# First layer of an MLP's last three parts as seven half-size products per pair of output tiles, on one Trainium2 core

## The chip, the cores and the metric

The kernel runs on one NeuronCore of one Trainium2 (trn2) chip. The metric is device time in microseconds (us) of one execution, smaller being better. The kernel before was timed three times: 862.24 us in the median, 861.46 to 862.5 us.

## What is computed

One inference step of a one-layer hybrid encoder, for a prompt of 512 tokens and a sample of 64 tokens (576 tokens together, 1024 channels): a modulated norm, an input projection, sparse attention beside a convolution, an output projection with a residual, and then the MLP, which is all that the change touches:

```
h = rms_norm(x, norm2_g) * (1 + sc2) + sh2
x = x + g2 * (jnp.square(jax.nn.relu(h @ w_ff1)) @ w_ff2)
...
y = rms_norm(x, final_g)
```

w_ff1 is 1024 x 4096, w_ff2 is 4096 x 1024, and sc2, sh2 and g2 come from the conditioning, one value per channel for the prompt and one for the sample. Everything is float32.

## The kernel before

**Float32 as three products.** A float32 operand is split into a high part, which is the value rounded to the matmul's 32-bit format (a copy on ScalarE, ACT), and a low part, the difference (a subtraction). A product is then three matmuls: high by high, high by low, low by high (`mm3`, lines 289 to 292). Matmul lines 290 to 292 therefore carry nearly all of the TensorE (PE) work.

**Layout.** Channels lie on the partitions, tokens along the free dimension, in two halves of 288 tokens (`JS`). An output tile is 128 channels by 288 tokens and takes one PSUM bank. Eight banks are shared out by tag: three `acc`, two `lg`, one `av`, which the MLP uses in rotation (`p_ff`), and two `tp`.

**The MLP in four parts.** Each part takes 1024 of the 4096 hidden channels. The first layer (`first_layer`, `ff1`, `ff1_evac`) makes eight hidden tiles: per tile 8 blocks of channels, 3 matmuls each, for two token halves, so 48 matmuls; the second layer makes eight output tiles from the eight hidden tiles, again 48 matmuls each, and adds them into the residual `x1` (`residual`, line 1087). In the last part the second layer runs over 320 and then 256 tokens, with the final norm behind it.

**Normalization folded behind the product.** The first layer multiplies the not yet normalized operand `h2` (the residual times the channel's scale). `h2` carries two extra columns with the shift, so one half has 290 columns. The evacuation then multiplies by the token's scale `rbc` on VectorE (DVE, line 1262), applies the shift as a bias in the ReLU on ACT (line 1266), squares into PSUM on ACT (line 1267), and makes high and low parts of the hidden tile `a` on DVE (lines 110 and 115).

**Weights.** `fetch` (line 318) issues a 512 KB DMA from SyncE (SP) into one of three `wraw` buffers, in the fixed sequence `order`. `split` (line 325) makes the high part in two copies of 128x512 on ACT (line 106) and the low part in two subtractions of 128x512 on GpSimd (POOL, line 332); `whi` and `wlo` have two buffers each. `take` fetches one tile, hands out a tile that is ready and splits the next one.

**What sets the order.** In the MLP the order of PE, ACT, DVE and POOL is the order in which the program is written (a manual schedule); each engine runs its own instructions in that order and waits for what it needs. The evacuation defers its last steps through `owed` and `settle`.

Of the kernel before, what the change touches and what calls it, by code (L numbers as in the profile page):

```python
# [7 lines left out]
FT = mybir.dt.float32  # L8
FR = mybir.dt.float32r
# [47 lines left out]
def f(ap):  # L57
    return ap.bitcast(FT)


def pump(g, n):
    for _ in range(n):
        next(g, None)
# [8 lines left out]
def step_kernel(ctx: ExitStack, tc: tile.TileContext, io):  # L72
# [25 lines left out]
    def p_tp():  # L98
        return bank("tp", 2)
# [14 lines left out]
    def sub(eng, out, a, b):  # L114
        eng.tensor_tensor(out, a, b, op=OP.subtract)
# [199 lines left out]
        order += [f_rows(w_ff2, 128 * KP * part, 128 * m) for m in range(NK)]  # L315
    stay = []

    def fetch():
        if order:
            raw = wgt.tile([128, 1024], FT, name="wraw", tag="wraw", bufs=3)  # L320
            src = order.pop(0)
            nc.sync.dma_start(raw.rearrange("p (k c) -> p k c", k=src.shape[1]), src)
            raws.append(raw)

    def split():
        if raws:
            raw = raws.pop(0)
            hi, lo = stay.pop(0)() if len(stay) > len(raws) + len(order) else [
                wgt.tile([128, 1024], FR, name=nm, tag=nm, bufs=2) for nm in ("whi", "wlo")]
            for c in (slice(0, 512), slice(512, 1024)):  # L330
                copy_to(act, hi[:, c], raw[:, c])
                behind[0] = pool.tensor_tensor(lo[:, c], raw[:, c], f(hi[:, c]), op=OP.subtract).ins  # L332
            ready.append((hi, lo))

    def take():
# [846 lines left out]
    ffp = new_pool(late, "ff")  # L1182

    def ft_(shape, dt, name):
        return ffp.tile(shape, dt, name=name, tag="d", bufs=21)

    mlp = ExitStack()
    mlp.enter_context(tc.manual_schedule(engines={mybir.EngineType.PE, mybir.EngineType.Activation, mybir.EngineType.DVE,
# [12 lines left out]
    def settle():  # L1201
        while owed:
            owed.pop(0)()
# [31 lines left out]
    def weight():  # L1235
        return [w.rearrange("p (k c) -> p k c", k=NK) for w in take()]
# [8 lines left out]
    def ff1(ts, parts=(range(NK),)):  # L1245
        w = weight()
        for ks in parts:
            for j in (1, 0):
                if j not in ts:
                    ts[j] = p_ff()[:, :HALF + 2 * j]  # L1250
                group(ts[j], w, h2, JX[j], ks)
            yield
# [21 lines left out]
        half(0)  # L1274
        return a

    def first_layer(part):
        a_ = []
        if part == 0:
            t0, t1 = {}, {}  # L1280
            g = ff1(t0, (FRONT, LAST))
            scales = spread(s2, 1.0 / D, rbc, dg)
            next(g)
            pump(scales, 1)
            pump(g, 2)
            pump(ff1(t1), 2)
            pump(scales, 2)
            a_ += [ff1_evac(t0), ff1_evac(t1)]
        while len(a_) < KP:
            t = {}  # L1290
            pump(ff1(t), 2)
            a_.append(ff1_evac(t))
        settle()
        return a_

# [7 lines left out]
            residual(t, r, m, G2)  # L1303

    for part in range(NP_ - 1):
        a_ = first_layer(part)
        for m in range(NK):
            ws = {m: weight()}
            if m == 0:
                second_layer(ws, (m,), a_, JS[::-1])  # L1310
            else:
                for r in JS:
                    t = p_ff()[:, :HALF]
                    group(t, ws[m], a_, r, range(NK))
                    residual(t, r, m, G2)

    def kept(m):
        if m < 4:
            return [big.tile([128, 1024], FR, name="wl", tag="b") for _ in range(2)]
        return [ft_([128, 1024], FR, "wl") for _ in range(2)]  # L1320
    stay += [lambda m=m: kept(m) for m in range(NK)]
    a_ = first_layer(NP_ - 1)


    fg = ft_([128, D], FT, "fg")
# [33 lines left out]
    for m in range(2, NK):  # L1359
# [1 line left out]
        t = p_ff()[:, :320]  # L1361
        group(t, ws[m], a_, LS[0], range(NK))
        residual(t, LS[0], m, G2)
    ys = [big.tile([128, D], FT, name="y", tag="b") for _ in range(2)]
    for m in range(NK):
        t = p_ff()[:, :TOK - 320]
        group(t, ws[m], a_, LS[1], range(NK))
# [43 lines left out]
```

## Time and profile before

| what | value |
|---|---|
| median of three runs | 862.24 us |
| the profiled execution's own time | 860.36 us |
| its span, first to last instruction | 858.6 us |
| PE busy, share of span | 94% |
| DVE, ACT, POOL busy | 52%, 48%, 35% |
| mean granted TensorE clock | 0.973 |

The profiled execution is one run on the chip; its time is 1.76 us more than its span and 1.88 us less than the median. Busy times are sums of instruction durations with overlaps counted once; matmuls are pipelined, so a matmul's own duration is longer than the distance from one to the next. A row of a group gives line, engine, operation, output and input with shapes, count, then busy time, mean duration, and the idle time of the engine before it with what ended it.

### The profile page before, as it was taken

How to read it: one execution, taken by the hardware profiler on the slowest of the kernel's cores; microseconds unless marked ns; L12 is line 12 of the kernel's file. 1: busy time of each engine (PE TensorE's matmuls, PEld its weight loads, DVE VectorE, ACT ScalarE, POOL GpSimd, SP SyncE). 2: the span in 40 equal slices, each digit the busy share in tenths (PEclk: the TensorE clock that was granted, in tenths of full speed). 3: DMA queues.
4: the chain of work that ended last, by engine and by line, in shares of the span. 5: the costliest groups of instructions: out<-in, count | busy, mean ns of one | idle time of the engine just before them, and what ended most of it. 6: DMA issues, size and time to landing. Idle time of an engine off the chain costs nothing.

```text
span 858.6 us, 17186 instructions
## 1 busy us (share of the span) xinstructions
PE 808.2 (94%) x6787; PEld 753.0 (88%) x6787; DVE 449.0 (52%) x1148; ACT 412.5 (48%) x976; POOL 303.5 (35%) x337
## 2 busy tenths in 40 slices
PE   5998997989798999999999999999999999999995
PEld 3797895567777988989999999999999999999995
DVE  4569879999997444654934311343113321144142
ACT  5365554555776787754745411443224522244332
POOL 0146342222244414232424343343433343343800
PEclk8799999899999999999999999999999999999998
DMA  8984157247343343732222323223222323223312
GB/s 241 309 205 123 53 146 184 60 100 187 112 113 110 116 137 115 222 122 77 74 74 75 97 76 93 80 75 99 74 77 82 88 83 90 74 74 101 120 55 57
DMA packets 164555, 95.57 MB, mean 111 GB/s; under 512 B 7699, under 2 KB 161119, under 8 KB 164475
## 3 DMA queue, kind: packets, MB, share of 16 engines
q1 hardware_dynamic: 164475, 94.48, 39.2%
q8 instruction: 53, 0.87, 0.4%
q14 instruction: 27, 0.22, 0.1%
HBM read 88.82 MB, written 5.64 MB: 110 GB/s over the span
## 4 chain that ended last, share of the span: by engine, by line
PE 69%; DVE 17%; ACT 7%; DMA 3%; issue 3%; POOL 1%; SPq 0%; ACTq 0%; DVEq 0%; POOLq 0%
PE ps_acc L290 11%; PE ps_acc L291 11%; PE ps_acc L292 11%; PE ps_lg L292 5%; PE ps_lg L290 5%; PE ps_lg L291 5%; DVE yc L564 3%; PE ps_av L292 3%; PE ps_av L290 2%; PE ps_av L291 2%; DVE score L690 2%; DVE m L688 2%; PE ps_tp L234 2%; DMA ada<-w_ada 1%; PE ps_av L887 1%
## 5 line engine op out<-in xcount | busy, mean ns | idle before, releaser
L332 POOL TENSOR_TENSOR wlo<-wraw,whi 128x512 fp32r<-128x512 f32 x172 | 222.6, 1314 | 378.3 <-ACT whi L106 378.0
L290 PE MATMUL ps_acc<-h,whi 128*128 128x288 f32 (+1 forms) x608 | 190.8, 314 | 0.0
L291 PE MATMUL ps_acc<-h,whi 128*128 128x288 f32 (+1 forms) x608 | 181.7, 299 | 0.0
L292 PE MATMUL ps_acc<-h,wlo 128*128 128x288 f32 (+1 forms) x608 | 181.1, 298 | 0.0
L106 ACT ACTIVATE whi<-wraw 128x512 fp32r<-128x512 f32 x172 | 99.8, 621 | 126.4 <-issue 120.6
L290 PEld LDWEIGHTS ps_acc<-h,whi 128*128 128x128 f32 x608 | 116.2, 191 | 14.3 <-issue 12.4
L291 PEld LDWEIGHTS ps_acc<-h,whi 128*128 128x128 f32 x608 | 116.7, 192 | 0.8
L292 PEld LDWEIGHTS ps_acc<-h,wlo 128*128 128x128 f32 x608 | 116.3, 191 | 0.0
L1266 ACT ACTIVATE z<-z,bs 128x224 f32<-128x224 f32 (+2 forms) x96 | 40.2, 450 | 98.6 <-DVE z L1262 98.6
L1087 DVE SCALAR_TENSOR_TENSOR x<-ps_acc,mod,x 128x288 f32<-128x288 f32 (+3 forms) x91 | 36.2, 420 | 83.6 <-PE ps_acc L292 83.0
L564 DVE SCALAR_TENSOR_TENSOR yc<-u,cw,yc 128x606 f32<-128x606 f32 x60 | 58.4, 981 | 0.6
L292 PE MATMUL ps_acc<-a,wlo 128*128 128x288 f32 x192 | 56.7, 295 | 0.0
L290 PE MATMUL ps_acc<-a,whi 128*128 128x288 f32 x192 | 56.6, 295 | 0.0
L291 PE MATMUL ps_acc<-a,whi 128*128 128x288 f32 x192 | 56.6, 295 | 0.0
L292 PE MATMUL ps_lg<-h,wlo 128*128 128x288 f32 (+1 forms) x176 | 52.2, 296 | 0.8 <-POOL wlo L332 0.8
L291 PE MATMUL ps_lg<-h,whi 128*128 128x288 f32 (+1 forms) x176 | 52.2, 297 | 0.0
L290 PE MATMUL ps_lg<-h,whi 128*128 128x288 f32 (+1 forms) x176 | 52.2, 296 | 0.1
L747 ACT ACTIVATE gc<-sful,sg 128x544 bf16<-128x544 f32 x48 | 35.8, 746 | 28.6 <-DVE sg L745 27.8
L872 POOL TENSOR_SCALAR prob<-prob,mx 128x128 f32<-128x128 f32 (+3 forms) x32 | 20.2, 631 | 56.8 <-DVE mx L871 34.2
L1087 DVE SCALAR_TENSOR_TENSOR x<-ps_lg,mod,x 128x64 f32<-128x64 f32 (+4 forms) x34 | 12.7, 407 | 52.5 <-PE ps_lg L292 52.5
L292 PE MATMUL ps_lg<-a,wlo 128*128 128x288 f32 x128 | 37.8, 295 | 0.0
L290 PE MATMUL ps_lg<-a,whi 128*128 128x288 f32 x128 | 37.8, 295 | 0.0
(358 smaller groups left out, 2019.0 us busy)
## 6 DMA issues: line engine op xcount, KB each, us to landing
wraw<-w_ff SPq DMA_DIRECT2D x64, 512.0 KB
ada<-w_ada SPq DMA_DIRECT2D x44, 512.0 KB
wraw<-w_in SPq DMA_DIRECT2D x24, 512.0 KB
wraw<-w_out SPq DMA_DIRECT2D x8, 512.0 KB
rep<-ud SPq DMA_DIRECT2D x24, 115.0 KB
xtok<-x_prompt SPq DMA_DIRECT2D x4, 512.0 KB
ada<-w_ada SPq DMA_DIRECT2D x8, 256.0 KB
ct<-cache_k SPq DMA_DIRECT2D x8, 256.0 KB
```

What stands on the lines that cost most here:

```text
L106: act.activation(out, in_, AF.Copy, scale=1.0 if scale is None else scale)
L234: pe.matmul(t[r:r + 32, :w], lhsT=cs[:, 4 * kh + kk, :], rhs=operand(v, kh, kk), start=kk == 0, stop=kk == 3, tile_position=(0, r))
L290: pe.matmul(out, lhsT=hi, rhs=src[:, 0, cs_], start=first, stop=False)
L291: pe.matmul(out, lhsT=hi, rhs=src[:, 1, cs_], start=False, stop=False)
L292: pe.matmul(out, lhsT=lo, rhs=src[:, 0, cs_], start=False, stop=last)
L332: behind[0] = pool.tensor_tensor(lo[:, c], raw[:, c], f(hi[:, c]), op=OP.subtract).ins
L564: dve.scalar_tensor_tensor(yc[c], src, w, yc[c], op0=OP.mult, op1=OP.add)
L688: dve.max(m, score[i])
L747: act.activation(eq, sful, AF.Sign, bias=cands[:, z:z + 1], scale=-1.0, accum_out=cnts[:, z:z + 1])
L872: pool.tensor_scalar(pt[:, :n], pt[:, :n], m[:, 1:2], 1.0, op0=OP.mult, op1=OP.mult)
L1087: dve.scalar_tensor_tensor(xm[:, a:b], t[:, a - r.start:b - r.start], mod[:, g, s, m:m + 1], xm[:, a:b], op0=OP.mult, op1=OP.add)
L1266: act.activation(y, y, AF.Relu, bias=bs[:, s:s + 1])
```

## The change

Of the four parts, the first keeps the old first layer, and the other three use a new one, `fast_layer`.

**Operands.** While part 0's first layer runs, `normalize` makes the normalized, scaled and shifted operand in float32 for four pairs of channel blocks (block i and block i+4). While part 0's second layer runs, `operands` forms, from each pair's four quarters (two channel blocks by two token halves), seven combinations: `11`, `12`, `22` are quarters, `s1` to `s4` sums and differences, each with high and low part. They stay in SBUF to the end.

**Products.** An output pair of tiles (256 hidden channels) by 576 tokens is computed as seven products of half size instead of eight (Strassen, in Winograd's form). A product is 4 channel blocks by 3 matmuls of 288 columns, 12 matmuls; a pair is 84. Products accumulate in banks `bk[0]`, `bk[1]`, `bk[4]`; some partial results are also added by DVE into other ones (`y3`, `u2`, a fourth bank `bk[5]`), and four half tiles come out, each through `made`: ReLU and square in place in PSUM, a high copy to SBUF, all on ACT, and a low subtraction on DVE.

**Weights.** `bring` takes two raw weight tiles, copies a quarter to a `tp` bank; `sums` makes four sums or differences on DVE (128x512, one operand in PSUM); `block` makes the high part of a product's weight on ACT and the low part on POOL (4 of 7) or DVE (3 of 7), three products ahead. A product's weight tile lies in one of four buffers.

**Other edits.** In part 0 a third tile's matmuls and its weight split are issued before the second tile is evacuated. Raw weight tiles also go to spare buffers (`spare`). Some splits make their second half's low part on DVE. The buffers of tag `d` go from 21 to 23, and some tiles of the last part change pools.

The diff, cut to what matters:

```diff
-                behind[0] = pool.tensor_tensor(lo[:, c], raw[:, c], f(hi[:, c]), op=OP.subtract).ins
+                behind[0] = (second[0] if c.start else pool).tensor_tensor(lo[:, c], raw[:, c], f(hi[:, c]), op=OP.subtract).ins
...
-        return ffp.tile(shape, dt, name=name, tag="d", bufs=21)
+        return ffp.tile(shape, dt, name=name, tag="d", bufs=23)
...
+    def normalize(i):
+        full[i] = ft_([128, 2, TOK], FT, "full")
+        for z in range(2):
+            m, y = i + 4 * z, full[i][:, z]
+            dve.tensor_tensor(y, x1[m // 2][:, m % 2], rbc, op=OP.mult)
+            for r, s in ((slice(0, SEQ), 0), (S, 1)):
+                act.activation(y[:, r], y[:, r], AF.Identity, scale=mod[:, SC2, s, m:m + 1], bias=mod[:, SH2, s, m:m + 1])
+    def operands():
+        for n, o in enumerate(OPS):
+            ops[o] = [big.tile([128, 2, TOK], FR, name="op", tag="b") if 2 * n + e < 9 else ft_([128, 2, TOK], FR, "op")
+                      for e in range(2)]
+        for i in range(4):
+            a11, a21 = full[i][:, 0, JS[0]], full[i][:, 0, JS[1]]
+            a12, a22 = full[i][:, 1, JS[0]], full[i][:, 1, JS[1]]
+            t = ft_([128, 4, HALF], FT, "sums")
+            c = slice(HALF * (i % 2), HALF * (i % 2) + HALF)
+            def put(o, src):
+                x = ops[o][i // 2]
+                copy_to(act, x[:, 0, c], src)
+                sub(dve, x[:, 1, c], src, f(x[:, 0, c]))
+            dve.tensor_tensor(t[:, 0], a21, a22, op=OP.add)
+            sub(dve, a21, a11, a21)
+            sub(dve, t[:, 1], t[:, 0], a11)
+            sub(dve, t[:, 2], a12, t[:, 1])
+            yield
+            put("11", a11)
+            put("12", a12)
+            yield
+            put("22", a22)
+            put("s3", a21)
+            yield
+            put("s1", t[:, 0])
+            put("s2", t[:, 1])
+            put("s4", t[:, 2])
+            yield
+    def bring(q):
+        b0, b1 = raws.pop(0), raws.pop(0)
+        x = p_tp()
+        copy_to(act, x, b1[:, :512])
+        pairs[q] = [b0[:, :512], b0[:, 512:], b1[:, :512], b1[:, 512:], x]
+    def sums(q, n):
+        if n == 2:
+            pairs[q].append(p_tp())
+        b11, b21, b12, b22, x, *y = pairs[q]
+        out, u, v = ((b12, b22, x), (x, x, b11), (y and y[0], b22, x), (y and y[0], b21, y and y[0]))[n]
+        sub(dve, out, u, v)
+    def block(g):
+        q, b = g // 7, g % 7
+        b11, b21, b12, b22, x, y = pairs[q] if len(pairs[q]) == 6 else pairs[q] + [None]
+        src = (b11, y, b21, b12, x, y, b22)[b]
+        nm = ("whi", "wlo")[g % 2]
+        w = blocks[g] = wgt.tile([128, 1024], FR, name=nm, tag=nm, bufs=2).rearrange("p (z c) -> p z c", z=2)
+        copy_to(act, w[:, 0], src)
+        return lambda: sub(dve if b in (1, 4, 5) else pool, w[:, 1], src, f(w[:, 0]))
+    MOVING = ("11", "s2", "12", "s3", "s1", "22", "s4")
+    def early(n):
+        if n == 0:
+            bring(0)
+            sums(0, 0)
+            sums(0, 1)
+        else:
+            sums(0, 2)
+            for g in range(2):
+                block(g)()
+    def made(q, a, r):
+        act.activation(q, q, AF.Relu)
+        act.activation(q, q, AF.Square)
+        copy_to(act, a[:, 0, r], q)
+        owed.append(lambda: sub(dve, a[:, 1, r], q, f(a[:, 0, r])))
+    def fast_layer():
         a_ = []
-        if part == 0:
-            t0, t1 = {}, {}
-            g = ff1(t0, (FRONT, LAST))
-            scales = spread(s2, 1.0 / D, rbc, dg)
-            next(g)
-            pump(scales, 1)
-            pump(g, 2)
-            pump(ff1(t1), 2)
-            pump(scales, 2)
-            a_ += [ff1_evac(t0), ff1_evac(t1)]
+        end = 7 * (KP // 2)
+        bk = old = None
+        for g in range(end + 2):
+            q, s = g // 7, g % 7
+            if s == 0:
+                old, bk = bk, {}
+            if g < end:
+                if s in (0, 1, 4):
+                    bk[s] = p_ff()[:, :HALF]
+                t = bk[(0, 1, 0, 1, 4, 1, 4)[s]]
+                w, x = blocks.pop(g), ops[MOVING[s]]
+                for k in range(4):
+                    c = slice(128 * k, 128 * k + 128)
+                    r = slice(HALF * (k % 2), HALF * (k % 2) + HALF)
+                    for n, (z, y) in enumerate(((0, 0), (0, 1), (1, 0))):
+                        pe.matmul(t, lhsT=w[:, z, c], rhs=x[k // 2][:, y, r], start=s in (0, 1, 4) and k + n == 0,
+                                  stop=k == 3 and n == 2, skip_group_check=True)
+            if s == 1 and g < end:
+                bk["y"] = mt([128, 2, HALF], FT, "y3")
+                copy_to(act, bk["y"][:, 0], bk[0])
+            todo = [block(h) for h in ((2, 3) if g == 0 else (g + 3,)) if h < end]
+            if s == 0 and old:
+                dve.tensor_tensor(old[4], old[4], old["u"], op=OP.add)
+                settle()
+                made(old[1], a_[-2], JS[1])
+            if s == 1 and old:
+                settle()
+                made(old[4], a_[-1], JS[0])
+            if g >= end:
+                continue
+            if s == 1:
+                sums(q, 3)
+            if s == 2:
+                bk["u"] = mt([128, 2, HALF], FT, "u2")[:, 0]
+                dve.tensor_tensor(bk["u"], bk[1], bk["y"][:, 0], op=OP.add)
+            if s == 3:
+                a_ += [ft_([128, 2, TOK], FR, "a") for _ in range(2)]
+                made(bk[0], a_[-2], JS[0])
+                late_ = owed.pop()
+            if s == 4:
+                dve.tensor_tensor(bk["y"][:, 1], bk[1], bk["y"][:, 0], op=OP.add)
+                owed.append(late_)
+            if s == 5:
+                bk[5] = p_ff()[:, :HALF]
+                dve.tensor_tensor(bk[5], bk[4], bk["y"][:, 1], op=OP.add)
+            if s == 6:
+                made(bk[5], a_[-1], JS[1])
+                late_ = owed.pop()
+                dve.tensor_tensor(bk[1], bk[1], bk["y"][:, 0], op=OP.add)
+                owed.append(late_)
+            if s in (2, 4):
+                settle()
+            if q + 1 < KP // 2 and s in (2, 3, 4):
+                if s == 2:
+                    bring(q + 1)
+                for n in {2: (), 3: (0, 1), 4: (2,)}[s]:
+                    sums(q + 1, n)
+            for e in todo:
+                e()
+            if s == 4:
+                fetch()
+                if q < KP // 2 - 2:
+                    fetch(spare)
+            if q == KP // 2 - 1 and s == 5:
+                second[0] = dve
+                split()
+                second[0] = pool
+        settle()
+        return a_
+    def weight2(m):
+        if m < NK - 2:
+            return weight()
+        fetch()
+        fetch(spare)
+        w = ready.pop(0)
+        if m == NK - 2:
+            split()
+        return [v.rearrange("p (k c) -> p k c", k=NK) for v in w]
+    def first_layer():
...
+        a_ = [ff1_evac(t0)]
+        t2 = {}
+        pump(ff1(t2), 2)
+        a_ += [ff1_evac(t1), ff1_evac(t2)]
         while len(a_) < KP:
             t = {}
             pump(ff1(t), 2)
             a_.append(ff1_evac(t))
+            if len(a_) in (4, 5, 6, 7):
+                normalize(len(a_) - 4)
...
-        a_ = first_layer(part)
+        a_ = fast_layer() if part else first_layer()
+        prep = iter(()) if part else operands()
         for m in range(NK):
-            ws = {m: weight()}
+            ws = {m: weight2(m)}
             if m == 0:
                 second_layer(ws, (m,), a_, JS[::-1])
+                pump(prep, 2)
             else:
                 for r in JS:
                     t = p_ff()[:, :HALF]
                     group(t, ws[m], a_, r, range(NK))
                     residual(t, r, m, G2)
+                    pump(prep, 1 + (m < 3))
+                    if m == NK - 2 + (r is JS[0]) and m >= NK - 2:
+                        early(m - NK + 2)
 
...
-    a_ = first_layer(NP_ - 1)
+    a_ = fast_layer()
+    second[0] = dve
```

## Rows read from the trace of the kernel before

**Rows 1.** The page: span, and busy time and share of each engine.

```profile
span 858.6 us, 17186 instructions
...
PE 808.2 (94%) x6787; PEld 753.0 (88%) x6787; DVE 449.0 (52%) x1148; ACT 412.5 (48%) x976; POOL 303.5 (35%) x337
```

**Rows 2.** Stretches: us, busy us (count) per engine, PE clock, DMA share, GB/s.

```profile
449.00:487.00 38.00, 37.11 (x276) 36.63 (x276) 18.12 (x50) 20.59 (x47) 15.31 (x12) 1.00 0.28 80
...
537.50:588.90 51.40, 51.40 (x387) 51.40 (x385) 19.59 (x54) 23.89 (x54) 20.44 (x16) 1.00 0.28 79
588.90:640.00 51.10, 51.10 (x388) 51.10 (x387) 10.78 (x28) 10.94 (x20) 20.60 (x17) 1.00 0.31 87
...
820.00:858.00 38.00, 29.15 (x241) 28.18 (x239) 15.21 (x42) 11.50 (x33) 0.00 (x0) 0.94 0.20 63
```

**Rows 3.** Waits, 437 to 860 us: total us, times, longest us.

```profile
PEld ps_lg L292 <- POOL wlo L332: 1.1, 1, 1.1
...
PE ps_lg L292 <- POOL wlo L332: 0.8, 1, 0.8
...
PEld ps_lg L290 <- ACT whi L106: 0.3, 1, 0.3
```

**Rows 4.** DVE in order of time: start us, us, instruction, idle before, releaser.

```profile
501.93 0.52 DVE L1087 SCALAR_TENSOR_TENSOR x<-ps_acc,mod,x 128x288 f32<-128x288 f32 x1 [2.55 <-PE ps_acc L292]
...
508.30 0.52 DVE L1087 SCALAR_TENSOR_TENSOR x<-ps_acc,mod,x 128x288 f32<-128x288 f32 x1 [2.55 <-PE ps_acc L292]
...
540.25 0.45 DVE L1262 TENSOR_TENSOR z<-ps_acc,rbc 128x288 f32<-128x288 f32 x1
...
588.30 0.46 DVE L1262 TENSOR_TENSOR z<-ps_av,rbc 128x288 f32<-128x288 f32 x1 [1.81 <-PE ps_av L292]
```

**Rows 5.** Groups of ACT instructions by line and shape.

```profile
L106 ACT ACTIVATE whi<-wraw 128x512 fp32r<-128x512 f32 x172 | 99.8, 621 | 126.4 <-issue 120.6 <-PE ps_acc L291 4.8 <-PE ps_lg L291 0.6
L1266 ACT ACTIVATE z<-z,bs 128x288 f32<-128x288 f32 x32 | 17.1, 536 | 56.6 <-DVE z L1262 56.6
...
L1267 ACT ACTIVATE ps_acc<-z 128x288 f32<-128x288 f32 x32 | 13.3, 415 | 1.0
...
L106 ACT ACTIVATE kv<-ps_acc 128x288 f32<-128x288 f32 x16 | 6.5, 405 | 2.8 <-DVE ksn L115 1.3 <-DVE kst L115 1.2
...
L106 ACT ACTIVATE kT<-ps_tp 128x512 fp32r<-128x512 f32 x8 | 4.7, 593 | 0.4 <-PE ps_tp L924 0.4
```

**Rows 6.** ACT in order of time in part 1's first layer.

```profile
543.85 0.54 ACT L1266 ACTIVATE z<-z,bs 128x288 f32<-128x288 f32 x1 [1.95 <-DVE z L1262]
544.42 0.42 ACT L1267 ACTIVATE ps_acc<-z 128x288 f32<-128x288 f32 x1
544.77 1.14 ACT L106 ACTIVATE whi<-wraw 128x512 fp32r<-128x512 f32 x2
```

**Rows 7.** Groups of DVE instructions by line and shape.

```profile
L115 DVE TENSOR_TENSOR a<-ps_acc,a 128x288 fp32r<-128x288 f32 x32 | 14.6, 457 | 1.1
...
L115 DVE TENSOR_TENSOR kT<-ps_tp,kT 128x512 fp32r<-128x512 f32 x8 | 5.5, 686 | 3.2 <-ACT kT L106 3.0
...
L1041 DVE TENSOR_TENSOR yc<-yc,csum 128x576 f32<-128x576 f32 x4 | 2.8, 752 | 0.3 <-ACT csum L106 0.3
```

**Rows 8.** Line 332: ns min/median/max, first and last start us.

```profile
L332 POOL TENSOR_TENSOR wlo<-wraw,whi x172: 1262/1295/1850, 54.1 to 783.3; 128x512 fp32r<-128x512 f32 x172
```

**Rows 9.** A late weight DMA: its issue on SP, its first reader.

```profile
797.50 0.37 SPq L322 DMA_DIRECT2D wraw<-w_ff  x1
...
802.33 1.15 ACT L106 ACTIVATE wl<-wraw 128x512 fp32r<-128x512 f32 x2 [4.89 <-DMA wraw<-w_ff]
```

**Rows 10.** Two stretches ahead of the MLP, columns as in rows 2.

```profile
129.00:150.00 21.00, 15.72 (x168) 11.57 (x166) 20.69 (x67) 9.12 (x23) 4.72 (x6) 1.00 0.74 186
...
215.00:236.00 21.00, 16.17 (x135) 15.18 (x136) 19.45 (x43) 16.81 (x45) 5.59 (x5) 0.92 0.41 115
```

More of the change, by code (lines that the diff above doesn't have):

```diff
@@ L316, in step_kernel, with fetch @@
     stay = []
-    def fetch():
+    def fetch(home=None):
         if order:
-            raw = wgt.tile([128, 1024], FT, name="wraw", tag="wraw", bufs=3)
+            raw = home() if home else wgt.tile([128, 1024], FT, name="wraw", tag="wraw", bufs=3)
             src = order.pop(0)
@@ L323, in fetch @@
             raws.append(raw)
+    second = [pool]
     def split():
@@ L1275, in ff1_evac @@
         return a
-    def first_layer(part):
-        a_ = []
-        if part == 0:
-            t0, t1 = {}, {}
-            g = ff1(t0, (FRONT, LAST))
-            scales = spread(s2, 1.0 / D, rbc, dg)
-            next(g)
-            pump(scales, 1)
-            pump(g, 2)
-            pump(ff1(t1), 2)
-            pump(scales, 2)
-            a_ += [ff1_evac(t0), ff1_evac(t1)]
+    full = [None] * 4
+    OPS = ("11", "12", "22", "s1", "s2", "s3", "s4")
+    ops = {}
+    def normalize(i):
[5 more added lines that the diff above has]
+                act.activation(y[:, r], y[:, r], AF.Identity, scale=mod[:, SC2, s, m:m + 1], bias=mod[:, SH2, s, m:m + 1])
@@ new lines, in step_kernel @@
+    pairs, blocks = {}, {}
+    def bring(q):
[17 more added lines that the diff above has]
+        return lambda: sub(dve if b in (1, 4, 5) else pool, w[:, 1], src, f(w[:, 0]))
@@ new lines, in spare @@
+    def spare():
+        return ft_([128, 1024], FT, "wraw2")
+    def weight2(m):
[8 more added lines that the diff above has]
+    def first_layer():
+        t0, t1 = {}, {}
+        g = ff1(t0, (FRONT, LAST))
+        scales = spread(s2, 1.0 / D, rbc, dg)
+        next(g)
+        pump(scales, 1)
+        pump(g, 2)
+        pump(ff1(t1), 2)
+        pump(scales, 2)
+        a_ = [ff1_evac(t0)]
+        t2 = {}
+        pump(ff1(t2), 2)
+        a_ += [ff1_evac(t1), ff1_evac(t2)]
@@ L1315, in step_kernel @@
                     residual(t, r, m, G2)
+                    pump(prep, 1 + (m < 3))
+                    if m == NK - 2 + (r is JS[0]) and m >= NK - 2:
+                        early(m - NK + 2)
     def kept(m):
-        if m < 4:
+        if m >= 4:
             return [big.tile([128, 1024], FR, name="wl", tag="b") for _ in range(2)]
@@ L1363, in step_kernel @@
         residual(t, LS[0], m, G2)
-    ys = [big.tile([128, D], FT, name="y", tag="b") for _ in range(2)]
+    ys = [ft_([128, D], FT, "y") for _ in range(2)]
     for m in range(NK):
```

## The prediction, made before the changed kernel ran

> **What bounds the kernel now.** I read the page first: TensorE (PE) is busy for 94% of the span, every other engine for about half or less [rows 1]. An average over the span says nothing of the MLP, so next came the table of stretches. In part 1's first layer PE is busy for 51.40 of 51.40 us, in the second layer behind it for 51.10 of 51.10, both at a granted clock of 1.00, which is the 2.4 GHz level; ACT and DVE reach 23.89 and 19.59 us in the first layer and 11 us in the second [rows 2]. Then the waits: between 437 us and the end of the MLP PE hardly waits for another engine, and the one place that matters is in part 0, 0.3 us for a high part and 0.8 to 1.1 us for a low part of a weight tile [rows 3]. So the MLP is a row of matmuls without gaps, and a matmul taken out there is worth its distance to the next one, as long as the other engines keep up.
>
> That distance comes from DVE's readers, which start when a group of matmuls has ended. In a second layer 48 matmuls of 288 columns lie between two residuals, 508.30 - 501.93 = 6.37 us, so 0.1327 us each. In part 1's first layer 15 half tiles lie between the first and last evacuation, 588.30 - 540.25 = 48.05 us, so 3.203 us a half tile (one half has 290 columns) and 16 x 3.203 = 51.25 us a part [rows 4].
>
> **The change, part by part.**
>
> *PE, parts 1 to 3.* Eight half tiles by two become four pairs of seven products of 12 matmuls: 336 matmuls in place of 384, all of 288 columns. 336 x 0.1327 = 44.6 us in place of 51.25: **6.65 us a part, 20.0 us in three parts**, if PE never waits. A pair takes 84 x 0.1327 = 11.15 us, a product 1.59 us; a pair took 12.81 us before.
>
> *ACT in the loop.* A pair needs seven high parts of 128x512 (four from SBUF at 0.621 us, three from PSUM at 0.593), `bring`'s copy (about 0.6, its form is close to these), `y3` (PSUM to SBUF, 288 wide, 0.405) and four times `made` [rows 5]. Its ReLU and square work in place in PSUM, which the trace does not show. From below, the nearest row is the PSUM read of the same width, 0.405, or the PSUM write, 0.415; from above, ReLU out of SBUF with a bias per partition, 0.536 [rows 5]. I take 0.41, since the bias and the SBUF read are what differ; ACT then waits about 0.03 us between dependent steps (543.85 + 0.54 to 544.42), and two independent copies take 1.14 us, not 1.24 [rows 6]. The sum is 2.48 + 1.78 + 0.6 + 0.41 + 12 x 0.41 + 8 x 0.03 = 10.4 us, 9.5 where neighbours overlap; with 0.536 for all twelve of `made` it is 11.9. Against 11.15 us of PE, ACT is nearly full but not the bound, at the value taken. The Trainium skill, Perfetto Trace Analysis, Optimizing Scalar/DVE Operations, gives ScalarE a smaller fixed access cost on PSUM (about 51 ns) than on SBUF (about 93 ns); by it, as an estimate, a step in place takes 0.04 us less than the 0.415 out of SBUF, and the sum is 10.1 instead of 10.4. The trace has 0.415 into PSUM and 0.405 out of it, no step in place.
>
> *DVE and POOL in the loop.* DVE: four sums and three low parts of 0.686, four low parts of the hidden tiles at 0.457, five additions of like width: 7 x 0.686 + 9 x 0.457 = 8.9 us of 11.15 [rows 7]. Writes into PSUM by DVE have no row; nearest are these reads, and 0.1 us more on each would still give 10.2. POOL: four low parts of 1.30, 5.2 us [rows 8].
>
> *The tightest wait.* A full sum is not enough, since the engines run in order. The product with s=3 overwrites a bank that DVE must have added into `u2` first. DVE's addition stands behind the low part of block 4, that behind ACT's copy of the block, and that behind `y3`, which follows, from the start of s=6: a block copy, `made`, a block copy, `made`, 3.75 us. So `y3` ends at about 4.35 us (s=2, which needs it, starts at 4.78), the block copy at 4.95, the low part at 5.65, `u2` at 6.1 plus latencies; s=3 starts at 4 x 1.59 = 6.37. The slack is **some 0.25 us, 0.5 where neighbours overlap**, and the other two waits (before s=5 and s=6) have about 0.9. I count no wait here.
>
> *Part 0.* The third tile's matmuls now come ahead of the second evacuation, so the split of the fourth weight tile leaves ACT's queue about 2 to 3 us earlier. The wait of 0.3 + 0.8 = **1.1 us** goes [rows 3] (bounds 0 and 1.4); the next split stands behind two evacuations and is still done about 1 us before it is needed. `normalize` puts two DVE multiplications of 0.752 [rows 7] and four ACT instructions behind an evacuation, on a tile of 6.4 us that ACT fills with about 3.5. As rows for those four I take 0.536 [rows 5] stretched to 512 columns, 0.8, and about 0.4 for 64 columns: 2.4 us. The next tile's split then ends on POOL some 0.3 us before PE wants it: taken as nothing, up to 2 us if each of four tiles is late by 0.5.
>
> *Making the operands.* 44 DVE instructions of about 0.45 us (20 us) and 28 ACT copies (12 us) lie in part 0's second layer, where DVE and ACT are idle for 40 of 51 us [rows 2]. They are late only for part 1, one tile and a half later. What is queued behind them on DVE are residuals, whose banks come round after five other groups (16 us). Nothing counted; 2 us if the cover fails.
>
> *Weights, and DMA.* A pair needs two tiles, 1 MB in 11.15 us, 94 GB/s against 79 now. SP waits only for buffers, and a late fetch was read 4.8 us after its issue [rows 9]; two at once, at most 9.6 us, are asked for five products (8 us) or more ahead, and the buffers come free earlier than that. Nothing counted, 1.5 us a pair if SP is held to the last moment.
>
> *Ends of a layer.* The second layer begins with 18 matmuls (2.4 us) on tiles long done; the last low parts come about 1.4 and 2.5 us after the last product, the latter needed only after 5.5. At the start, the first two weight blocks are made during part 0's last half tile. The last part's splits get DVE's help, and PE already waits little there. Behind the last product nothing of the tail's 38 us changes [rows 2].
>
> **Sum.** 20.0 + 1.1 = 21.1 us. Against the profiled execution, 860.36 - 21.1 = 839.3; its time lies 1.88 us under the median, so on the median's scale **841.1 us**.
>
> **Rivals.**
>
> *ACT becomes the bound.* If the in-place steps cost 0.536, or each instruction carries 0.1 us more, ACT needs 11.5 to 11.9 us a pair, the slack before s=3 is gone and PE waits at s=2, 3, 5 and 6. For it speaks that no row shows the in-place form and that ACT stands at 93% of the loop; against it the PSUM rows. Time: (12.81 - 11.7) x 12 = 13.3 us saved, with part 0 14, so **about 848 us**, 843.5 to 853 with the bounds.
>
> *GpSimd and DVE lock each other out.* `normalize` and `operands` are DVE instructions with both inputs in SBUF, put beside POOL's 12 splits of that stretch. Line 332 has instances of 1.85 us against 1.30 in the median, so something does stretch POOL [rows 8]; the trace does not say what. If both split instructions of the four tiles with `normalize` are held by that 0.55 us, the low part is late by 1.1 less the 0.3 of slack, four times: 3 us, **844 us**. In the loop itself all DVE operands pair PSUM with SBUF, so it ends there. The Trainium skill, SBUF — State Buffer, Who interferes with whom, says just this, an exclusive lock between a GpSimd read and a DVE instruction with two SBUF inputs; by it the whole cost is this stretch, and no row here isolates it.
>
> *Slower: the clock falls.* If PE waits in each product, the granted clock might leave 1.00 in the three layers. At the 1.2 GHz level a matmul takes twice as long, and a pair reaches 12.81 us, the time before, when about 15% of its matmuls run there (11.15 x 1.15 = 12.8); at a quarter it is 13.9 us, 12 x 1.1 = 13 us lost and **about 874 us**. Against it: in stretches where PE idled for a quarter of the time, busy for 15.72 of 21 us, the clock was 1.00, and for 16.17 of 21 it was 0.92 [rows 10]. Waits of a few tenths at a product fall far short of that, and even the dearest ACT sum, 11.9, is under 12.81.
>
> *No gain.* Were the distance of two matmuls stretched by the change of weights and banks every 12 matmuls by 0.14 us a product, a pair would lose 1 us; every 24 matmuls, where bank and reader change now, no such gap is in the 0.1327. Only 1.66/7 = 0.24 us a product would cancel the gain: 862 us.
>
> **How the numbers follow.** The forecast 0.62, ACT as the bound 0.25, the lock 0.06, slower 0.04, no gain 0.03. The forecast's own range is 838.5 to 843.5 (1.4 for 1.1 in part 0 and a little on the median below; normalize, operands or a wait of 0.2 us a pair above). The range, 838.5 to 850, takes in that, the lock and two thirds of ACT as the bound, so it leaves out under 2 in 10. A measurement of this kernel can tell about 0.2% (1.7 us) from no change; faster by more than that 0.93, within it 0.03, slower 0.04.
>
> **What would show it.** In the stretches, each new first layer should last about 44.6 us, PE busy throughout at 1.00, ACT busy 38 to 42 us, DVE 32 to 36. In the waits, no lines of PE or its weight loads for `y3`, `u2` or a weight block above a few tenths of a us in all; lines that return 12 times speak for ACT as the bound, and their releaser names the chain. The mean of the ReLU and square in place decides the term that is weakest, and part 0's wait should be gone. I am wrong if the first layers last over 46 us, or if something else in part 0 or the tail grows by over 2 us.

## The result, and the profile after

The changed kernel takes **838.29 us** in the median of four runs (837.84 to 839.02), the kernel before, on the same chip, 861.85 us (861.33 to 862.5): a ratio of 0.9727, 95% interval [0.971, 0.9744], so faster, by 23.6 us of medians. 841.1 was forecast with a range from 838.5: the mechanism forecast is the one that acted, and the time lies 0.2 us below the range.

The page of the changed kernel's profiled execution, which took 837.84 us (before: [rows 1]):

```profile
span 836.1 us, 17187 instructions
...
PE 784.3 (94%) x6643; PEld 729.7 (87%) x6643; DVE 526.7 (63%) x1234; ACT 465.2 (56%) x1104; POOL 296.8 (36%) x327
```

The share of PE is what it was; PE is busy for less time, DVE and ACT for more. The stretches, with the columns of [rows 2]: part 0's first layer, its second layer, part 1's first layer, its second layer, and the tail.

```profile
447.00:485.00 38.00, 38.00 (x287) 38.00 (x286) 24.09 (x59) 30.21 (x67) 15.27 (x12) 1.00 0.25 70
485.00:534.00 49.00, 49.00 (x372) 49.00 (x371) 38.25 (x73) 20.12 (x47) 22.42 (x15) 1.00 0.39 108
534.00:578.50 44.50, 44.50 (x338) 44.50 (x337) 31.10 (x60) 33.89 (x77) 20.69 (x16) 1.00 0.26 72
578.50:629.50 51.00, 51.00 (x387) 51.00 (x386) 12.50 (x30) 12.08 (x23) 19.09 (x15) 1.00 0.37 104
...
797.00:836.00 39.00, 29.63 (x245) 28.66 (x243) 15.23 (x42) 11.49 (x33) 0.00 (x0) 0.95 0.20 61
```

The new first layer fits into 44.5 us where the old one took 51.4. PE is busy for all of it at a granted clock of 1.00, with ACT at 33.89 and DVE at 31.10 us beside it (the prediction named 38 to 42 and 32 to 36 as signs; part of a layer's work on ACT lies ahead of it and behind it). Part 0's second layer, into which the operands were put, is full on PE too, although DVE went to 38 us there.

The waits from 430 to 840 us, columns as in [rows 3], hold little between part 0 and the end of the last part:

```profile
PE ps_lg L1523 <- DVE x L1089: 1.1, 3, 0.6
...
PE ps_av L292 <- POOL wl L334: 0.4, 1, 0.4
...
PEld ps_av L292 <- POOL wl L334: 0.6, 1, 0.6
```

The first belongs to the tail. Part 0's waits on a weight tile are gone, and no line names `y3`, `u2` or a weight block. One wait has grown, on the low part of a weight of the last second layer: its load waits 0.6 us, and PE 0.4. Before, the load alone waited:

```profile
PEld ps_av L292 <- POOL wl L332: 0.4, 1, 0.4
```

**A ledger by stage.** To see where 23.6 us come from I cut both traces at DVE events that exist in both. The reciprocal just ahead of the MLP and the last residual, before:

```profile
437.88 0.19 DVE L1004 RECIPROCAL rs<-rs 128x5 f32<-128x5 f32 x1 [4.34 <-ACT rs L1003]
...
849.24 0.61 DVE L1087 SCALAR_TENSOR_TENSOR x<-ps_lg,mod,x 128x192 f32<-128x192 f32 x2 [2.15 <-PE ps_lg L292]
```

and after, with the last residual of part 0, the first layer's last addition of parts 1 and 3, and the first residual of part 3 between:

```profile
437.40 0.19 DVE L1006 RECIPROCAL rs<-rs 128x5 f32<-128x5 f32 x1 [4.75 <-ACT rs L1005]
...
534.93 0.64 DVE L1089 SCALAR_TENSOR_TENSOR x<-ps_lg,mod,x 128x224 f32<-128x224 f32 x2 [0.59 <-PE ps_lg L292]
...
579.36 0.47 DVE L1395 TENSOR_TENSOR ps_acc<-ps_acc,u 128x288 f32<-128x288 f32 x1 [0.86 <-PE ps_acc L1388]
...
769.99 0.47 DVE L1395 TENSOR_TENSOR ps_acc<-ps_acc,u 128x288 f32<-128x288 f32 x1 [1.12 <-PE ps_acc L1388]
...
777.23 0.55 DVE L1089 SCALAR_TENSOR_TENSOR x<-ps_acc,mod,x 128x320 f32<-128x320 f32 x1 [1.32 <-PE ps_acc L292]
...
826.73 0.61 DVE L1089 SCALAR_TENSOR_TENSOR x<-ps_lg,mod,x 128x192 f32<-128x192 f32 x2 [2.14 <-PE ps_lg L292]
```

A first layer after, for one, is 579.36 - 534.93 = 44.43 us. The whole table, in us:

| from, to | before | after | gain |
|---|---|---|---|
| start to the reciprocal ahead of the MLP | 437.88 | 437.40 | 0.48 |
| reciprocal to part 0's last evacuation | 48.12 | 46.65 | 1.47 |
| first layers, parts 1, 2, 3 | 51.36, 51.36, 51.34 | 44.43, 44.42, 44.42 | 20.79 |
| first layer's end to first residual, parts 0, 1, 2 | 5.98, 5.97, 5.97 | 5.96, 5.97, 5.95 | 0.04 |
| the same, part 3 | 6.98 | 7.24 | -0.26 |
| first to last residual, parts 0, 1, 2 | 44.96, 44.86, 45.01 | 44.92, 44.96, 44.91 | 0.04 |
| the same, part 3 | 49.45 | 49.50 | -0.05 |
| last residual to the end of the execution | 11.12 | 11.11 | 0.01 |
| whole MLP, reciprocal to last residual | 411.36 | 389.33 | **22.03** |

The two profiled executions are 860.36 - 837.84 = 22.52 us apart: 0.48 ahead of the MLP, 22.03 in it, 0.01 behind it. Since the MLP is the only place that the change touches, it is worth 22 us by the traces; the medians' 23.6 holds something else, which the repeats below name.

### The profile page after: what moved, and what is told of

Its sections match the earlier page's. It is cut to its first block, busy times and chain, and to the rows that moved or that the text cites. A ratio compares the mean times of both kernels' runs of the same rounds, so it can differ in the third digit from the quotient of the medians.

```text
span 836.1 us, 17187 instructions
## 1 busy us (share of the span) xinstructions
PE 784.3 (94%) x6643; PEld 729.7 (87%) x6643; DVE 526.7 (63%) x1234; ACT 465.2 (56%) x1104; POOL 296.8 (36%) x327
## 4 chain that ended last, share of the span: by engine, by line
PE 67%; DVE 18%; ACT 7%; issue 4%; DMA 2%; POOL 1%; SPq 0%; ACTq 0%; DVEq 0%; POOLq 0%
PE ps_acc L290 9%; PE ps_acc L291 8%; PE ps_acc L292 8%; PE ps_acc L1388 8%; PE ps_lg L1388 4%; DVE yc L566 4%; PE ps_lg L290 3%; PE ps_lg L292 3%; PE ps_lg L291 3%; DVE score L692 3%; DVE m L690 2%; PE ps_av L1388 2%; PE ps_tp L234 2%; PE ps_av L292 2%; PE ps_av L290 2%
## 5 line engine op out<-in xcount | busy, mean ns | idle before, releaser
L334 POOL TENSOR_TENSOR wlo<-wraw,whi 128x512 fp32r<-128x512 f32 x122 | 162.6, 1351 | 271.1 <-ACT whi L106 268.4
L290 PE MATMUL ps_acc<-h,whi 128*128 128x288 f32 (+1 forms) x416 | 133.7, 322 | 0.0
L291 PE MATMUL ps_acc<-h,whi 128*128 128x288 f32 (+1 forms) x416 | 124.4, 299 | 0.0
L292 PE MATMUL ps_acc<-h,wlo 128*128 128x288 f32 (+1 forms) x416 | 124.2, 299 | 0.0
L290 PEld LDWEIGHTS ps_acc<-h,whi 128*128 128x128 f32 x416 | 80.0, 192 | 14.3 <-issue 12.7
L291 PEld LDWEIGHTS ps_acc<-h,whi 128*128 128x128 f32 x416 | 80.0, 192 | 0.9
L292 PEld LDWEIGHTS ps_acc<-h,wlo 128*128 128x128 f32 x416 | 79.8, 192 | 0.0
L115 POOL TENSOR_TENSOR whi<-wraw,whi 128x512 fp32r<-128x512 f32 x24 | 31.1, 1295 | 52.3 <-ACT whi L106 51.1
L115 POOL TENSOR_TENSOR wlo<-wraw,wlo 128x512 fp32r<-128x512 f32 x24 | 31.1, 1294 | 34.4 <-ACT wlo L106 32.5
L1388 PE MATMUL ps_acc<-op,whi 128*128 128x288 f32 x264 | 38.5, 295 | 0.0
L1388 PE MATMUL ps_acc<-op,wlo 128*128 128x288 f32 x264 | 38.5, 295 | 0.0
L291 PE MATMUL ps_lg<-a,whi 128*128 128x288 f32 x128 | 37.7, 295 | 0.0
L290 PE MATMUL ps_lg<-a,whi 128*128 128x288 f32 x128 | 37.7, 295 | 0.0
```

Source lines behind the costliest of these rows:

```text
L290: pe.matmul(out, lhsT=hi, rhs=src[:, 0, cs_], start=first, stop=False)
L291: pe.matmul(out, lhsT=hi, rhs=src[:, 1, cs_], start=False, stop=False)
L292: pe.matmul(out, lhsT=lo, rhs=src[:, 0, cs_], start=False, stop=last)
L334: behind[0] = (second[0] if c.start else pool).tensor_tensor(lo[:, c], raw[:, c], f(hi[:, c]), op=OP.subtract).ins
L1388: pe.matmul(t, lhsT=w[:, z, c], rhs=x[k // 2][:, y, r], start=s in (0, 1, 4) and k + n == 0, stop=k == 3 and n == 2, skip_group_check=True)
```

## The experiments

Unless said otherwise the times are medians of four or more runs, each with its ratio to the kernel before on the same chip, and "the MLP" is the last line of the ledger, taken from that run's trace.

**The changed kernel again.** No edit; it asks how far the two numbers repeat.

> The changed kernel once more, unedited, timed over more runs. Theory 'scale': a profiled execution stands at no fixed distance from the median, so the medians of more runs differ by what the two traces differ by, 22.5 us, give or take 0.6, and this kernel's median comes to 838.3 to 839.3. Rival 'size': the sum itself was too small by over 2 us in every execution; then the medians differ by 23.5 us or more, again.

838.57 us over 5 runs (836.79 to 838.88), against 861.27 over 17 runs of before (859.36 to 862.25): 0.9731 [0.9717, 0.9745], 22.7 us. Its MLP takes 389.32 us, 0.01 from the first trace. Over the 13 traces of this study the reciprocal ahead of the MLP stands anywhere between 436.5 and 439.6 us, though nearly every edit lies behind it; the two traces of this one kernel have it at 437.40 and 438.21. So, as far as these traces tell, the runs of one kernel differ by their first 437 us; with 17 runs of before the medians' difference falls to within 0.7 us of the ledger's 22.03.

**Part 0's order, alone in before, and undone in after.** In the kernel before:

```diff
-            a_ += [ff1_evac(t0), ff1_evac(t1)]
+            a_ += [ff1_evac(t0)]
+            t2 = {}
+            pump(ff1(t2), 2)
+            a_ += [ff1_evac(t1), ff1_evac(t2)]
```

> The kernel before with the third tile's matmuls and split issued ahead of the second evacuation in part 0, and nothing else of the change. Theory: the waits for the fourth weight tile go, 1.1 to 1.5 us off the kernel before (about 860.6 us), and the waits of PE for POOL and ACT near 452 us are gone from its trace. Rival: what part 0 gained in the changed kernel's trace is drift between executions; then the time is that of before within 0.5 us.

and the reverse in the changed kernel:

> The changed kernel with that order of part 0 put back (both tiles evacuated before the third is issued). Theory: 1.1 to 1.5 us slower than the changed kernel, with the wait back at the same place. Rival: under the changed kernel's other work in part 0 the order is worth nothing (0 within 0.5 us) or, by the instructions of normalize behind each evacuation, over 2 us.

Alone it gives 859.71 us over 12 runs, 0.998 [0.9971, 0.9989]; the MLP falls by 1.40 us, from 411.36 to 409.96, nearly all of it in part 0 (48.12 to 46.70). Undone in after, 841.25 us, 0.9764 [0.9752, 0.9777]; the MLP grows by 1.49 to 390.82, and these waits are back:

```profile
PE ps_lg L292 <- POOL wlo L334: 0.8, 1, 0.8
...
PEld ps_lg L292 <- POOL wlo L334: 1.1, 1, 1.1
...
PEld ps_lg L290 <- ACT whi L106: 0.3, 1, 0.3
```

The step is worth 1.4 to 1.5 us, which is 0.3 + 1.1: the line of the weight load, not PE's 0.8, measures this stop. In after, with `normalize` in it, part 0 lasts 46.65 us against 46.70 without it: `normalize` costs nothing.

**The price of the two shift columns.** The new operand contains the shift, so no half tile has 290 columns. To price that alone, before was run with 288 columns throughout; this leaves the shift out of the first layer's operand.

```diff
-    JX = (slice(0, HALF), slice(HALF, TOK + 2))
+    JX = JS
...
-                    ts[j] = p_ff()[:, :HALF + 2 * j]
+                    ts[j] = p_ff()[:, :HALF]
...
-        copy_to(dve, bs, ts[1][:, HALF:HALF + 2])
+        copy_to(dve, bs, ts[1][:, HALF - 2:HALF])
```

> The kernel before without the two extra columns of the first layer's moving operand (it leaves out the shift sh2), so that every matmul of the first layer has 288 columns. It sizes the part of the change that is the normalized operand alone. Theory: the halves of 290 columns took 3.23 us against 3.19, so a part's first layer gets 0.3 us shorter, 51.36 to 51.0, 1.3 us over four parts. Rival: the first layer's matmuls are as far apart with 288 columns (0.1337), and the difference to the new layer's 0.1322 has another cause; then a part stays within 0.1 us of 51.36.

859.6 us over 7 runs, 0.9977 [0.9964, 0.9989]; a first layer takes 50.99, not 51.36. So 0.37 us of a part's gain of 6.93 come from columns, and the other 6.56 from the rest, 48 matmuls fewer above all (48 x 50.99 / 384 = 6.37).

**Room on ACT: place against sum.** The prediction put the danger into ACT, once as a sum (10.4 of 11.15 us a pair) and once as a place (the chain `y3`, block copy, low part, `u2` ahead of s=3, where s is a product's number in its pair, 0 to 6). Three kernels add independent copies of 128x288 on ACT (0.44 us each) to the loop: four a pair in the chain's way (two ahead of `y3`, two between it and the block copy), the same four behind it, or one in every product, seven a pair.

```diff
+    dum = ffp.tile([128, HALF], FT, name="dum", tag="dum", bufs=1)
...
+            for _ in range(2 if g < end and s in (0, 1) else 0):
+                act.activation(dum, dum, AF.Copy)
             todo = [block(h) for h in ((2, 3) if g == 0 else (g + 3,)) if h < end]
```

That is the first; the second has `s in (4, 5)`, the third `range(1 if g < end else 0)`.

> The changed kernel with two more ACT instructions (288 columns, in place on a tile of their own, about 0.4 us each) in each product s=0 and s=1 of every pair, so 1.4 to 1.7 us more ACT work a pair, placed ahead of the copy y3 and of block 4. Theory 'slack': in the changed trace y3 ends 0.8 us and u2 0.6 us before PE needs them, so PE now waits 0.8 to 1.1 us a pair at s=2 and s=3, 10 to 13 us in all. Rival 'load': ACT is at about 8.5 of 11.1 us a pair, so 1.7 us more fit and the time stays within 1 us.

> The same added ACT work, two instructions in each product s=4 and s=5 of every pair. Theory 'slack': ACT idles there for 1.8 us a pair waiting for a weight buffer, so nothing changes, within 1 us. Rival 'load': ACT is the bound as soon as work is added anywhere, then this costs as much as adding it at s=0 and s=1.

> The changed kernel with one more ACT instruction (0.44 us, on a tile of its own) in each of the seven products of a pair, 3.1 us more ACT work a pair. The loop without its seventh product settled at 10.47 us a pair with ACT idle for 1.4 of them, so ACT's own work is about 9.1 us. Theory 'sum': 9.1 + 3.1 = 12.2 us against 11.1, ACT becomes the bound and a pair takes 1.1 us more, 13 us in all, 852 us. Rival 'place': only the three instructions between s=6 and s=1 count, the rest fill the idle time at s=4 and s=5; then 0.3 to 0.5 us a pair, 842 to 845 us.

| copies a pair | us | ratio to before | a first layer, us | MLP, us |
|---|---|---|---|---|
| none | 838.57 | 0.9731 [0.9717, 0.9745] | 44.42 | 389.32 |
| four, s=0 and 1 | 848.65 | 0.9857 [0.9841, 0.9874] | 47.45 | 398.38 |
| four, s=4 and 5 | 839.13 | 0.9746 [0.9732, 0.9761] | 44.44 | 390.12 |
| seven, one each | 841.95 | 0.9773 [0.9757, 0.979] | 45.24 | 392.35 |

Thirty microseconds of part 1's first layer as one stretch, columns as in [rows 2], after:

```profile
545.00:575.00 30.00, 30.00 (x229) 30.00 (x228) 20.73 (x42) 25.22 (x61) 14.17 (x11) 1.00 0.25 71
```

with four copies in s=0 and 1:

```profile
545.00:575.00 30.00, 28.94 (x215) 28.14 (x213) 18.50 (x38) 25.78 (x62) 13.21 (x11) 1.00 0.19 54
```

with four in s=4 and 5:

```profile
545.00:575.00 30.00, 30.00 (x229) 30.00 (x228) 20.85 (x43) 28.08 (x69) 14.10 (x11) 1.00 0.29 80
```

and with seven:

```profile
545.00:575.00 30.00, 30.00 (x223) 29.46 (x222) 20.30 (x41) 28.83 (x73) 12.92 (x10) 1.00 0.20 58
```

ACT (fourth busy time) at 28.08 of 30 us costs the loop nothing, and at 25.78 of 30 it costs 3 us a layer: its busy share does not say what it costs. The place does, and the waits of the kernel with four copies in the chain's way name the chain, its last member the addition into `u2` (the two other banks have the same line):

```profile
PEld ps_lg L1390 <- DVE u L1411: 2.3, 3, 0.8
...
PEld ps_acc L1390 <- ACT y L106: 1.0, 6, 0.2
```

These are nine waits, not twelve: in a layer's first pair, where ACT has no pair before it to evacuate, the copies cost nothing. It ends 11.13 us after the last residual (536.83), the later ones 12.1 us apart, where the changed kernel has 11.11 for all four:

```profile
547.96 0.47 DVE L1399 TENSOR_TENSOR ps_acc<-ps_acc,u 128x288 f32<-128x288 f32 x1 [1.12 <-PE ps_acc L1390]
...
560.06 0.47 DVE L1399 TENSOR_TENSOR ps_acc<-ps_acc,u 128x288 f32<-128x288 f32 x1 [1.04 <-PE ps_acc L1390]
```

So a late chain costs 1.0 us in each of nine pairs, inside the 0.8 to 1.1 expected of one pair; the 10 to 13 us expected in all (9.06 came) had counted it in twelve. Copies in s=4 and 5 cost 0.8 us, nearly all of it once, where the last second layer starts (8.02 us for 7.24). The seven cost 0.2 to 0.4 us in each later pair, against 0.3 to 0.5 expected of place and far from the 1.1 of a full sum, though at 28.83 of 30 us ACT has next to nothing left.

**Six products.** The matmuls of the seventh product are left out, everything else stays, so that PE needs 72 x 0.1322 = 9.5 us a pair and the next bound comes up.

```diff
-                for k in range(4):
+                for k in range(4 if s < 6 else 0):
```

> The changed kernel without the 12 matmuls of every pair's seventh product (s=6); its weight block is still made, so the tiles that take this product lack one term. It shows what bounds the loop next. If PE alone is the bound, 12 x 1.59 = 19.1 us go, about 819 us. If ACT with its waits for weight buffers is close behind, a pair takes about 10 us instead of 9.5 and 12 to 14 us go, about 825 us, with waits of PE for ACT and DVE in every pair.

830.86 us, 0.9651 [0.9634, 0.9668]; the MLP is 7.24 us shorter, less than either expectation. A first layer takes 41.89 us: its first pair 9.9, the later ones 10.66, in each of which the weight load now waits about 1 us for `y3`:

```profile
PEld ps_acc L1388 <- ACT y L106: 5.7, 6, 1.0
...
PE ps_acc L1388 <- ACT y L106: 4.3, 6, 0.7
...
PE ps_lg L1388 <- ACT y L106: 2.1, 3, 0.7
```

So in the changed kernel PE is the bound by some 11.11 - 10.66 = 0.45 us a pair, and the next one is the order of work on ACT ahead of `y3`.

**The lock between DVE and GpSimd, in the loop.** The sums' intermediate tiles go from PSUM to SBUF, so that DVE reads two SBUF operands beside POOL.

```diff
-        x = p_tp()
+        x = ft_([128, 512], FT, "xs")
...
-            pairs[q].append(p_tp())
+            pairs[q].append(ft_([128, 512], FT, "ys"))
```

> The changed kernel with the two work tiles of bring and sums in SBUF instead of the tp banks, so that seven DVE instructions a pair have both inputs in SBUF, beside four POOL subtractions a pair. Theory 'lock': each that meets a POOL instruction lasts up to 1.55 instead of 0.69 us, as the late splits did; u2 comes up to 0.9 us later against 0.6 us of slack, and PE waits 0.3 to 1.3 us a pair, 4 to 15 us in all. Rival 'no lock in the loop': SBUF and PSUM operands cost DVE the same, 0.69 us, and the time stays within 1 us.

843.49 us, 0.9795 [0.978, 0.981]; the MLP is 3.73 us longer, just under the 4 to 15 expected, and a first layer takes 45.63. The three pairs in which the next pair's sums are made last 11.5 to 11.6 us, the last one 11.10. Groups of DVE instructions of part 1's first layer, columns as in [rows 7]:

```profile
L115 DVE TENSOR_TENSOR xs<-xs,wraw 128x512 f32<-128x512 f32 x3 | 5.0, 1670 | 0.1
...
L115 DVE TENSOR_TENSOR ys<-wraw,xs 128x512 f32<-128x512 f32 x3 | 3.1, 1042 | 0.0
...
L115 DVE TENSOR_TENSOR ys<-wraw,ys 128x512 f32<-128x512 f32 x3 | 2.0, 682 | 0.0
```

The same sums take 0.69 us with one operand in PSUM. Two of the four (the fourth, `wraw<-wraw,xs`, takes 0.682) are stretched to 1.04 and 1.67. POOL's subtractions mostly stay at 1.30, but some of them last 1.4 to 1.78. In two encounters the engine that began first kept its time, and the other was held:

```profile
529.55 0.68 DVE L115 TENSOR_TENSOR wraw<-wraw,xs 128x512 f32<-128x512 f32 x1
529.62 1.78 POOL L115 TENSOR_TENSOR whi<-wraw,whi 128x512 fp32r<-128x512 f32 x1 [3.35 <-ACT whi L106]
...
552.48 1.30 POOL L115 TENSOR_TENSOR wlo<-wraw,wlo 128x512 fp32r<-128x512 f32 x1 [3.50 <-ACT wlo L106]
...
552.66 1.67 DVE L115 TENSOR_TENSOR xs<-xs,wraw 128x512 f32<-128x512 f32 x1
```

In the pair around 552.66 PE was held not by `u2`, which the expectation named, but ahead of s=5. That this product is held by DVE's addition behind these sums (`y` at s=4) fits the times (it ends at 554.70, the load of s=5 follows at 554.82), but the profile names only "issue".

**The help of DVE in splits, and the start of the last second layer.** With the splits' second half back on POOL throughout:

```diff
-                second[0] = dve
+                second[0] = pool
...
-    second[0] = dve
```

> The changed kernel with POOL making both halves of each late split, as before, so DVE's help is undone. Theory 'lock': DVE's halves took 1.54 us beside POOL against 0.68 alone, so DVE's help ends hardly earlier than POOL alone would; 0 to 0.4 us either way. Rival 'help': PE's wait at the start of the last second layer grows from 0.4 to over 1 us, and the kernel is slower by that.

839.13 us, 0.9739 [0.9724, 0.9753], and an MLP of 389.32 us, the same to 0.01: that help is worth nothing. In the changed kernel POOL works beside DVE there, and both are stretched: two of DVE's low parts, at 772.83 and behind it, take 3.08 us together, where the one at 778.16 takes 0.68, and three of POOL's take 4.70, where 14 take 17.55 with POOL alone:

```profile
772.35 4.70 POOL L334 TENSOR_TENSOR wl<-wraw,wl 128x512 fp32r<-128x512 f32 x3 [4.87 <-ACT wl L106]
...
772.83 3.08 DVE L334 TENSOR_TENSOR wl<-wraw,wl 128x512 fp32r<-128x512 f32 x2 [0.58 <-ACT wl L106]
```

The 0.26 us that part 3 gives back lie where the split of the last layer's second weight stands, behind the last `made` on ACT. It was moved ahead:

```diff
                 late_ = owed.pop()
+                if stay and q == KP // 2 - 1:
+                    split()
```

> The changed kernel with the split of the last second layer's second weight tile issued in the last pair's s=6, ahead of the last two evacuations on ACT. Theory: the last second layer starts 0.26 us later against the layer before it than in the kernel before because that split stands behind the last evacuation; PE's wait of 0.4 to 0.6 us for the low part goes, and the stretch from the last product to the first residual falls from 7.24 to 6.7 to 6.9 us. Rival: the evacuations delayed by the split make PE wait instead, and the stretch stays or grows. The time alone can't tell 0.4 us; the trace can.

In the trace that start takes 778.78 - 772.17 = 6.61 us, where it took 7.24 (and 6.98 before), and the wait on `wl` is gone:

```profile
772.17 0.47 DVE L1395 TENSOR_TENSOR ps_acc<-ps_acc,u 128x288 f32<-128x288 f32 x1 [1.12 <-PE ps_acc L1388]
...
778.78 0.55 DVE L1089 SCALAR_TENSOR_TENSOR x<-ps_acc,mod,x 128x320 f32<-128x320 f32 x1 [0.48 <-PE ps_acc L292]
```

The MLP is 388.70 us, the shortest of all that compute everything. The median, 838.76 us (836.44 to 839.39), 0.9733 [0.9715, 0.9752], cannot tell 0.6 us.

## Why the prediction was nearly right, and where it failed

*PE, parts 1 to 3: right in kind, 0.28 us a part too small.* 6.65 us a part was forecast; from residual to residual parts 1 and 2 gained 6.93 and 6.96. The new layer's spacing is 44.43 / 336 = 0.1322, not 0.1327 (0.17 us), and the old one took 51.36 us, not 51.25 (0.11): 16 times the mean of the 15 later half tiles, where the first of a part takes 3.31. Part 3 gained 6.66 only, since 0.26 went at the start of the last second layer. "The last part's splits get DVE's help" counted that start at nothing; the help is void (389.32 us for the MLP without it, 389.33 with it), and the split stands behind the last `made`: moved ahead of it, the start took 6.61 for 7.24.

*Part 0: the wait is gone, as forecast, but worth 1.47.* It was taken at 0.3 + 0.8 with 1.4 as the bound; the traces with the edit alone and with it undone give 1.40 and 1.49, the sum with the weight load's 1.1.

*ACT in the loop: right.* The in-place steps, priced at 0.41 out of a PSUM write of 0.415 and a PSUM read of 0.405, take 0.395 to 0.406 in part 1's first layer:

```profile
L106 ACT ACTIVATE a<-ps_acc 128x288 fp32r<-128x288 f32 x7 | 2.9, 412 | 0.2
...
L1366 ACT ACTIVATE ps_acc<-ps_acc 128x288 f32<-128x288 f32 x7 | 2.8, 406 | 0.0
...
L1367 ACT ACTIVATE ps_acc<-ps_acc 128x288 f32<-128x288 f32 x7 | 2.8, 395 | 0.2
```

In the stretch of 30 us ACT is busy for 25.22, so 25.22 / 30 x 11.1 = 9.3 us a pair: the forecast's 9.5 with overlaps, not 10.4. The Trainium skill, Perfetto Trace Analysis, Optimizing Scalar/DVE Operations, puts ScalarE's fixed cost lower on PSUM than on SBUF. The rows here do not settle it: against 0.395 to 0.406 in place stands 0.415 out of SBUF [rows 5], but the kernel before has another square out of SBUF into PSUM, which the prediction passed over, at 0.394:

```profile
L1212 ACT ACTIVATE ps_tp<-x 128x288 f32<-128x288 f32 x16 | 6.3, 394 | 0.0
```

*The tightest wait: right that none comes, the slack too small.* In one pair PE's products start like this:

```profile
556.95 1.75 PE L1388 MATMUL ps_acc<-op,whi 128*128 128x288 f32 x12
558.53 1.75 PE L1388 MATMUL ps_av<-op,wlo 128*128 128x288 f32 x12
560.12 1.75 PE L1388 MATMUL ps_acc<-op,whi 128*128 128x288 f32 x12
561.71 0.56 PE L1388 MATMUL ps_av<-op,wlo 128*128 128x288 f32 x3
```

and the copy into `y3` and the addition into `u2` stand so:

```profile
558.95 0.41 ACT L106 ACTIVATE y<-ps_acc 128x288 f32<-128x288 f32 x1
```

```profile
560.66 0.45 DVE L1407 TENSOR_TENSOR u<-ps_av,y 128x288 f32<-128x288 f32 x1
```

`y3` ends 560.12 - 559.36 = 0.76 us ahead of s=2, `u2` 561.71 - 561.11 = 0.6 ahead of s=3; for `u2`, 0.25 to 0.5 was forecast. The chain is the one named: copies added in its way made PE wait for `u2`.

*Operands and `normalize`: right at nothing, with less cover than thought.* In part 0's second layer DVE was priced at about 0.45 us an instruction; the groups there show

```profile
L115 DVE TENSOR_TENSOR full<-full 128x288 f32<-128x288 f32 x4 | 4.8, 1188 | 0.1
...
L115 DVE TENSOR_TENSOR op<-sums,op 128x288 fp32r<-128x288 f32 x12 | 8.6, 772 | 0.0
```

so DVE came to 38 of 49 us, and PE still never waited.

*The rivals.* Neither ACT as the bound, nor a lower clock (1.00 in every layer), nor a gap at the change of banks (products stand 1.59 us apart) appeared. The lock exists, and where the change lets it act it costs nothing that the ledger shows. The Trainium skill, SBUF — State Buffer, Who interferes with whom, says that a GpSimd instruction that reads SBUF and a DVE instruction on two SBUF inputs exclude one another. The sums moved to SBUF and the late splits agree: DVE took up to 1.67 us for 0.69, POOL up to 1.78 for 1.30. The prediction let the lock end with part 0's operands, since in the loop DVE pairs PSUM with SBUF; it missed the late splits, where both of DVE's operands lie in SBUF.

*The step that failed: the sum's sizes, and the carry to the median.* The time missed by 841.14 - 838.29 = 2.85 us. The terms were too small by 22.03 - 21.1 = 0.93 us. The other 1.92 come from "its time lies 1.88 us under the median, so on the median's scale": that distance was taken as the kernel's own, though by the traces it is one execution's place in the drift of the first 437 us. The changed kernel's profiled execution was itself 0.48 us quicker there, 0.01 behind the MLP, and lay only 0.45 us under its median (0.48 + 0.01 + 1.88 - 0.45 = 1.92); over 17 runs before's median is 861.27, and the three runs at hand had lain high. The range's low end counted 0.3 us for part 0 and "a little on the median"; the drift alone moves a single run by more. It was missed by 0.2 us, and the five later runs' median, 838.57, would lie within it. What makes the spacing 0.1322 and not 0.1327 was not tried.

## What to carry to other kernels

Where a stretch of the trace shows PE without a gap, a removed matmul is worth its distance to the next, and one that swaps matmuls for ACT and DVE work keeps its gain as long as the longest chain ahead of a bank's reuse ends in time; look for that chain and its slack instead of adding busy shares, and put extra work behind it. Price a small change by the distance between two events of the same stage in both traces, and do not carry one execution's distance from the median to another kernel. Measure a stop by the longest line it has, the weight load's included, and give a stage's ends a line of their own.

## What was not expected of the hardware

The part ahead of the MLP drifts by 3 us between executions (436.5 to 439.6), while the 389 us of the MLP behind it differ by 0.01 between the two traces of the changed kernel. A DVE instruction with two SBUF inputs beside POOL took up to 2.4 times as long (1.67 us for 0.69); POOL, where DVE had begun first, took 1.78 for 1.30. The granted clock stayed at 1.00 over the first layers even where PE waited 0.5 us at a product in three of a layer's four pairs.
